# Paired column sums, bias rows on SP's queue and new rooms for accumulators in a two-layer decoder trunk

## The chip, the cores and the metric

The kernel runs on one core of a Trainium2 chip. The metric is the device time of one execution in microseconds (us). The program is compiled into one instruction stream for each engine: PE (TensorE: matrix products), DVE (VectorE), ACT (ScalarE), POOL (GpSimd) and SP (SyncE, which here only issues DMAs). An engine works through its own stream in order and waits at an instruction whose operands or whose output buffer are not ready.

## The reference

Two layers (D = 1024, 256 positions, hidden width 2816). Each layer is an FFN, a token mixer and a second FFN, and nine vectors of 1024 numbers, made from the conditioning vector `c`, modulate them. Vectors 0 and 1, 3 and 4, 6 and 7 are shift and scale of a norm; 2, 5 and 8 are the gates of the residual.

```
c_act = silu(c)
for l in range(2):
    mod = c_act @ w_ada[l] + b_ada[l]            # 9 vectors of 1024
    sh1, sc1, g1, sh2, sc2, g2, sh3, sc3, g3 = split(mod, 9)
    x = x + 0.5 * g1 * swiglu(rms_norm(x) * (1 + sc1) + sh1, ffn1_gate[l], ffn1_up[l], ffn1_down[l])
    x = x + g2 * token_mix(rms_norm(x) * (1 + sc2) + sh2, ...)
    x = x + 0.5 * g3 * swiglu(rms_norm(x) * (1 + sc3) + sh3, ffn2_gate[l], ffn2_up[l], ffn2_down[l])
return rms_norm(x) * final_norm
# swiglu(u, wg, wu, wd) = (silu(u @ wg) * (u @ wu)) @ wd
```

Everything is float32.

## The kernel before, in words

**Weights.** All weights stream in as `raw` tiles of 1 MB, issued by SP into four buffers (`raws`, bufs=4). A float32 weight is split in two: ACT copies it to `whi` (L177), DVE writes the remainder `wlo` (L179), and PE makes three products for each pair of operands: hi by hi, lo by hi and hi by lo. A `raw` buffer is free for the next load when its last reader is done: for a weight that is the second `wlo` split, for `w_ada` the last of DVE's four accumulations over it.

**FFN.** In the gate and up part, groups of 256 hidden columns follow each other (one `raw` tile of gate, one of up); DVE forms `hf` (L497) and its remainder `hl` (L499). In the down part two passes c = 0 and 1 run over six loads of `ffn_down`, each of which gives two *units*: one unit is one `whi` and one `wlo` of 128x1024 and twelve matmuls 128x512 of PE. At the end of a pass DVE adds the result to x (L455, L456, `rtmp`).

**Modulation.** The nine vectors are computed beside this work. A vector has two halves of 512 columns, a half has two loads of `w_ada` (1 MB each). `ada_half` issues them and lets DVE sum eight slices of 128x512 into a tile `acc` (L222 the first, L224 the others). For a gate the first of them adds the tile `binit`, whose row 0 holds the bias; that row of 2 KB is fetched by a DMA on ACT's queue (L212) in front of the half. What is left is a sum over the partitions, made by PE with a matrix of ones:

- a gate's half (a *row half*) is split into `acc0`, `acc1` (ACT L231, DVE L232), PE makes two matmuls 128x512 (`tr<-acc,ones`), ACT writes the gate `g` (L238);
- a half of a shift or scale (a *column half*) takes four matmuls of 32 columns in a bank `tr` (eight records in the trace), after which DVE picks the columns (L194 `mcol`, L197 `cs`) and adds the bias (L203 `col`).

`acc` has two buffers in the pool `keep`, which all halves use in turn. So a half can begin when PE has done the sums of the half before the last.

**Order.** `ada_step` goes one load further in this work; it is called between two loads of weights, once or twice for each group of the FFN and once for each load of `ffn_down`. The sums of a half are put one step after its last accumulation (`ada_late`). The tile framework's scheduler sets each engine's order at build time; at run time it is fixed.

The first two vectors of layer 0 and of layer 1's first FFN are made by another function. Layer 1's first FFN makes vectors 2, 3, 4 and 5 beside its groups and its down part: gate halves of vector 5 are summed in the down part.

Of the kernel before, what the change touches and what calls it, by code (L numbers as in the profile page):

```python
# [10 lines left out]
F32 = mybir.dt.float32  # L11
F32R = mybir.dt.float32r
AF = mybir.ActivationFunctionType
ALU = mybir.AluOpType
# [63 lines left out]
def hybrid_trunk(ctx, tc, t, out):  # L78
# [36 lines left out]
    pad(const, "before", 480)  # L115
# [4 lines left out]
    c_in = const.tile([P, KD], F32, name="c_in")  # L120
    nc.scalar.dma_start(c_in, t["c"].rearrange("o (p j) -> (o p) j", p=P))
    tab = const.tile([P, TAB_END], F32, name="tab")
# [3 lines left out]
    cact = const.tile([P, KD], F32, name="cact")  # L126
    nc.scalar.activation(cact, c_in, AF.Silu)
    apart = keep.tile([P, 48], F32, name="apart")
# [3 lines left out]
    pad(const, "behind", 352)  # L132
# [53 lines left out]
    def column_sums(ps, vec, a, start, stop):  # L186

        av = a.rearrange("p (j i r) -> p j i r", j=4, i=4)
        for i in range(4):
            mm(ps[32 * i:32 * i + 32, :P].rearrange("p (j r) -> p j r", j=4), vec, av[:, :, i, :], start, stop)  # L190

    def pick_columns(ps):
        m = small.tile([P, 4, 32], F32, name="mcol", tag="mcol", bufs=1)
        nc.vector.tensor_tensor(m, ps[:, :P].rearrange("p (j r) -> p j r", j=4),  # L194
                                colmask[:, None, :].to_broadcast([P, 4, 32]), ALU.mult)
        cs = small.tile([P, 4], F32, name="cs", tag="cs", bufs=2)
        nc.vector.tensor_reduce(cs, m, AX.X, ALU.add)  # L197
        return cs

    def add_bias(l, ch, n, cs):  # L200
        if (l, ch) not in mods:
            mods[l, ch] = small.tile([P, KD], F32, name="col", tag="col", bufs=8)
        nc.vector.scalar_tensor_tensor(mods[l, ch][:, n * 4:n * 4 + 4], cs, 1.0 if ch in (1, 4, 7) else 0.0,  # L203
                                       bcols[:, l, ch * 8 + n * 4:ch * 8 + n * 4 + 4], ALU.add, ALU.add)

    def ada_half(l, ch, n):
        acc = keep.tile([P, 512], F32, name="acc", tag="acc", bufs=2)
        row = ch in (2, 5, 8)
        n0 = ch * D + n * 512
        wv = t["w_ada"][l].rearrange("(p j) n -> p j n", p=P)  # L210
        if row:
            nc.scalar.dma_start(binit[0:1, :], t["b_ada"][l:l + 1, n0:n0 + 512])  # L212
        for j in range(0, KD, 4):
            r = raw_tile()
            rv = r.rearrange("p (j n) -> p j n", j=4)
            nc.sync.dma_start(rv, wv[:, j:j + 4, n0:n0 + 512])
            if ada_lag[0]:
                yield
            for jj in range(4):
                cj = cact[:, j + jj:j + jj + 1]  # L220
                if j + jj == 0 and not row:
                    nc.vector.tensor_scalar_mul(acc, rv[:, jj, :], cj)  # L222
                else:
                    nc.vector.scalar_tensor_tensor(acc, rv[:, jj, :], cj, binit if j + jj == 0 else acc,  # L224
                                                   ALU.mult, ALU.add)
            yield
        if row:
            if n == 0:
                mods[l, ch] = keep.tile([P, D], F32, name="g", tag="g", bufs=2)
            hi, lo = (scr.tile([P, 512], F32R, name="acc%d" % i, tag="uf", bufs=2) for i in range(2))  # L230
            nc.scalar.activation(hi, acc, AF.Copy)  # L231
            nc.vector.tensor_tensor(lo, acc, hi.bitcast(F32), ALU.subtract)  # L232

            def finish():
                ps = trps()
                mm(ps, ones, hi, True, False)
                mm(ps, ones, lo, False, True)
                nc.scalar.activation(mods[l, ch][:, n * 512:(n + 1) * 512], ps, AF.Copy, scale=1.0 if ch == 5 else 0.5)  # L238
        else:
            def finish():  # L240
                ps = trps()
                column_sums(ps, ones[:, :32].bitcast(F32), acc, True, True)
                cs = pick_columns(ps)
                add_bias(l, ch, n, cs)
        ada_late.append(finish)
# [5 lines left out]
    def ada_load(chunks):  # L251
        def g():
            for l, ch, n in chunks:
                for _ in ada_half(l, ch, n):
                    yield
                    while ada_late:
                        ada_late.pop(0)()
            while ada_late:
                ada_late.pop(0)()
        ada_gen[0] = g()  # L260
# [51 lines left out]
    def norm_mod(hf, uhi, ulo, sc, sh, by_act=False):  # L312
# [15 lines left out]
        def rest(bs=(0, 1)):  # L328
            for b in bs:
                uf = scr.tile([P, 4, P], F32, name="uf", tag="uf", bufs=2)  # L330
# [129 lines left out]
    def ffn(l, which, uhi, ulo, ada_plan, post, xn=None, side=None):  # L460
# [4 lines left out]
        with tc.tile_pool(name="ffn", bufs=1) as fp, tc.tile_pool(name="fu", bufs=EXTRA) as fu, \  # L465
# [7 lines left out]
            unit_alloc["f"] = lambda: pool_unit(fu)  # L473
            bank_pools[:] = [psum, fps]
# [26 lines left out]
            def begin():  # L501


                wa = t["w_ada"][l].rearrange("(p j) n -> p j n", p=P)
                cb = fp.tile([P, KD, 32], F32, name="cb", tag="sgx", bufs=2)
                nc.vector.tensor_copy(cb, cact[:, :, None].to_broadcast([P, KD, 32]))
# [40 lines left out]
                def operands(q):  # L547
                    cs = pick_columns(sums[q])
# [3 lines left out]
                    uf = scr.tile([P, 2, S], F32, name="uf", tag="uf", bufs=2)  # L552
# [64 lines left out]
            else:  # L617
                hidden()
                xs_group([(stream_units(wg[:, :, :512], KD, 512, 4, 2), 512, lambda hf, ps: gp.append(ps), 4),
# [29 lines left out]
            bank_pools[:] = [psum]  # L649


    def token_mix(l, uhi, ulo, ada_plan, post):
        uhk, ulk = ktiles(uhi), ktiles(ulo)
        w_in = t["w_in"][l].rearrange("(k p) n -> p k n", p=P)
        with tc.tile_pool(name="tm", bufs=1) as tp, tc.tile_pool(name="aps", bufs=2, space=PSUM) as aps:
# [58 lines left out]
            win = [scr.tile([P, 16, 2, 15], F32, name="win%d" % i, tag="uf", bufs=2) for i in range(2)]  # L714
# [259 lines left out]
            def transposed(blocks, eng):  # L974
# [4 lines left out]
                pT = scr.tile([P, 512], F32, name="pT", tag="uf", bufs=2)  # L979
# [142 lines left out]
    bcols = const.tile([P, DEPTH, 72], F32, name="bcols")  # L1122
# [18 lines left out]
    def final_norm(hf):  # L1141
        if hf == 0:
            for c in range(2):
                fnorm[c] = scr.tile([P, 512], F32, name="fnorm%d" % c, tag="uf", bufs=2)
# [18 lines left out]

    pad(scr, "before_uf", 320)
    pad(small, "behind_uf", 192)
# [57 lines left out]
```

## Time and profile before

| | |
|---|---|
| median of 3 runs | 1177.56 us (1176.16 to 1180.53) |
| the profiled execution | 1177.39 us, its span 1175.6 us |
| PE busy | 1145.2 us, 97% |
| DVE busy | 939.7 us, 80% |
| ACT busy | 642.8 us, 55% |
| granted TensorE clock | 0.999 |
| DMA on SP's queue | 273.02 MB, 70.8% of 16 engines' span |

Shares are means over stages that differ: what the change touches lies in the FFNs, and there the rows of single stretches count. A group of rows "x8" in a timeline is eight instructions in a row, its time from the start of the first to the end of the last. A matmul's time in the profile is modelled and overlaps the next; the pace of PE is read from the starts.

### The profile page before, as it was taken

How to read it: one execution, taken by the hardware profiler on the slowest of the kernel's cores; microseconds unless marked ns; L12 is line 12 of the kernel's file. 1: busy time of each engine (PE TensorE's matmuls, PEld its weight loads, DVE VectorE, ACT ScalarE, POOL GpSimd, SP SyncE). 2: the span in 40 equal slices, each digit the busy share in tenths (PEclk: the TensorE clock that was granted, in tenths of full speed). 3: DMA queues.
4: the chain of work that ended last, by engine and by line, in shares of the span. 5: the costliest groups of instructions: out<-in, count | busy, mean ns of one | idle time of the engine just before them, and what ended most of it. 6: DMA issues, size and time to landing. Idle time of an engine off the chain costs nothing.

```text
span 1175.6 us, 20207 instructions
## 1 busy us (share of the span) xinstructions
PE 1145.2 (97%) x7886; PEld 1005.6 (86%) x7886; DVE 939.7 (80%) x1889; ACT 642.8 (55%) x1156; POOL 2.6 (0%) x16
## 2 busy tenths in 40 slices
PE   4999999999999999999999999999999999999997
PEld 3799987799977889998879999777997788999985
DVE  4998899779888898799578879975888888865553
ACT  4544445647676564444455534365676757565441
POOL 0000000000000000000000000000000000000000
PEclk9999999999999999999999999999999999999999
DMA  9989999686723578988838979965574254986530
GB/s 329 333 294 318 329 342 354 203 231 184 220 80 104 193 232 297 314 290 318 287 108 289 321 266 347 342 230 165 154 225 114 88 180 143 294 267 210 188 135 36
DMA packets 201970, 274.95 MB, mean 234 GB/s; under 512 B 13613, under 2 KB 119815, under 8 KB 201875
## 3 DMA queue, kind: packets, MB, share of 16 engines
q1 hardware_dynamic: 201119, 273.02, 70.8%
q8 instruction: 62, 1.02, 0.4%
q10 hardware_dynamic: 756, 0.64, 0.2%
q14 instruction: 33, 0.27, 0.1%
HBM read 272.60 MB, written 1.05 MB: 233 GB/s over the span
## 4 chain that ended last, share of the span: by engine, by line
PE 64%; DVE 18%; DMA 11%; ACT 4%; issue 3%; SPq 1%; DVEq 0%; ACTq 0%
PE mm L105 55%; DVE wlo L179 8%; DMA raw<-in_ffn_up 6%; DVE acc L224 4%; PE tr L108 3%; DMA raw<-in_w_ada 3%; ACT whi L177 2%; PE sc L105 2%; PE po L105 2%; DMA raw<-in_ffn_down 1%; PE tr L105 1%; DVE win L728 1%; DMA raw<-in_ffn_gate 1%; DVE hf L497 1%; DVE rtmp L455 0%
## 5 line engine op out<-in xcount | busy, mean ns | idle before, releaser
L179 DVE TENSOR_TENSOR wlo<-raw,whi 128x1024 fp32r<-128x1024 f32 (+5 forms) x400 | 423.3, 1074 | 119.5 <-ACT whi L177 118.6
L177 ACT ACTIVATE whi<-raw 128x1024 fp32r<-128x1024 f32 (+5 forms) x400 | 364.4, 937 | 231.0 <-PE mm L105 92.8
L105 PE MATMUL mm<-uhi,whi 128*128 128x256 f32 x1248 | 346.6, 278 | 0.0
L105 PE MATMUL mm<-ulo,whi 128*128 128x256 f32 x1248 | 344.9, 276 | 0.0
L105 PE MATMUL mm<-uhi,wlo 128*128 128x256 f32 x1248 | 344.9, 276 | 0.0
L105 PEld LDWEIGHTS mm<-uhi,whi 128*128 128x128 f32 x1248 | 234.3, 188 | 2.7 <-issue 1.8
L105 PEld LDWEIGHTS mm<-ulo,whi 128*128 128x128 f32 x1248 | 234.5, 188 | 0.5
L105 PEld LDWEIGHTS mm<-uhi,wlo 128*128 128x128 f32 x1248 | 234.3, 188 | 0.0
L224 DVE SCALAR_TENSOR_TENSOR acc<-raw,cact,acc 128x512 f32<-128x512 f32 x224 | 167.3, 748 | 4.2 <-DMA raw<-in_w_ada 1.3
L105 PE MATMUL mm<-whi,hh 128*128 128x512 f32 x352 | 138.3, 393 | 0.0
L105 PE MATMUL mm<-wlo,hh 128*128 128x512 f32 x352 | 137.3, 390 | 0.7 <-DVE wlo L179 0.7
L105 PE MATMUL mm<-whi,hl 128*128 128x512 f32 x352 | 137.0, 389 | 0.0
L105 PE MATMUL mm<-whi,uhi 128*128 128x512 f32 (+3 forms) x336 | 126.4, 378 | 3.3 <-ACT uhi L557 2.6
L105 PE MATMUL mm<-whi,ulo 128*128 128x512 f32 (+3 forms) x336 | 126.0, 376 | 1.2 <-DVE ulo L345 1.2
L105 PE MATMUL mm<-wlo,uhi 128*128 128x512 f32 (+3 forms) x336 | 125.2, 373 | 0.0
L498 ACT ACTIVATE hh<-hf 128x256 fp32r<-128x256 f32 x70 | 29.3, 418 | 101.7 <-DVE hf L497 101.6
L105 PEld LDWEIGHTS mm<-whi,hh 128*128 128x128 f32 x352 | 66.1, 188 | 15.0 <-issue 1.4
L105 PEld LDWEIGHTS mm<-wlo,hh 128*128 128x128 f32 x352 | 66.1, 188 | 14.7 <-DVE wlo L179 1.4
L105 PEld LDWEIGHTS mm<-whi,hl 128*128 128x128 f32 x352 | 66.1, 188 | 13.8
L105 PEld LDWEIGHTS mm<-whi,uhi 128*128 128x128 f32 x336 | 63.3, 189 | 14.8 <-ACT uhi L557 3.3
L105 PEld LDWEIGHTS mm<-whi,ulo 128*128 128x128 f32 x336 | 63.7, 190 | 11.8 <-DVE ulo L345 2.9
L105 PEld LDWEIGHTS mm<-wlo,uhi 128*128 128x128 f32 x336 | 63.6, 189 | 9.4
(248 smaller groups left out, 1328.4 us busy)
## 6 DMA issues: line engine op xcount, KB each, us to landing
raw<-in_w_ada SPq DMA_DIRECT2D x72, 1024.0 KB, 7.9
raw<-in_ffn_gate SPq DMA_DIRECT2D x41, 1024.0 KB, 6.6
raw<-in_ffn_up SPq DMA_DIRECT2D x41, 1024.0 KB, 6.1
raw<-in_ffn_down SPq DMA_DIRECT2D x40, 1024.0 KB, 7.6
raw<-in_w_in SPq DMA_DIRECT2D x18, 1024.0 KB, 5.7
raw<-in_w_in SPq DMA_DIRECT2D x16, 512.0 KB, 4.7
raw<-in_w_out SPq DMA_DIRECT2D x8, 1024.0 KB, 5.4
raw<-in_ffn_down SPq DMA_DIRECT2D x8, 512.0 KB
```

Source lines behind the costliest of these rows:

```text
L105: last_mm[0] = nc.tensor.matmul(o, a, b, start=start, stop=stop)
L108: nc.tensor.transpose(o, a, ident)
L177: nc.scalar.activation(a, s, AF.Copy)
L179: nc.vector.tensor_tensor(b, s, a.bitcast(F32), ALU.subtract)
L224: nc.vector.scalar_tensor_tensor(acc, rv[:, jj, :], cj, binit if j + jj == 0 else acc, ALU.mult, ALU.add)
L497: nc.vector.tensor_tensor(hf32, ps[:, 256:], sg, ALU.mult)
L498: nc.scalar.activation(h[0][:, f, :], hf32, AF.Copy)
L728: nc.vector.tensor_tensor(win[i][jj * 64:(jj + 1) * 64, 8 * a:8 * a + 8, g, :], pv[g * 64:(g + 1) * 64, jj, :, a:a + 15], cols[0][jj * 64: ...
```

## The change

1. The two column halves of a vector are held and summed together: `column_sums` takes both accumulators and writes 256 columns of one bank, `mcol`, `cs` and `col` are made at double width, once for a vector. The sums come two steps after the second half; those of a row half one step after it, as before.
2. The bias row of a gate's half is fetched on SP's queue, by `bias_row`, which is called in the middle of the half before (for the first of all, in front of it). The tile `binit` is the same, so each fetch waits for DVE's accumulation that reads the row before it.
3. The accumulators of every second vector in an FFN (counter `pairs`, shift and scale only) go to a room of the FFN's pool, under the tag `sgx`, at other addresses; all others stay in `keep`'s two buffers. In the token mixer none goes there. With both halves held, a vector whose accumulators are in `keep` holds both buffers until its sums are done.
4. Tiles of the constants, `uf` and the paddings are laid out anew; SBUF offsets of some small tiles change.

```diff
-    def column_sums(ps, vec, a, start, stop):
-
-        av = a.rearrange("p (j i r) -> p j i r", j=4, i=4)
-        for i in range(4):
-            mm(ps[32 * i:32 * i + 32, :P].rearrange("p (j r) -> p j r", j=4), vec, av[:, :, i, :], start, stop)
...
+    def column_sums(ps, vec, halves):
+
+        for n, a in enumerate(halves):
+            av = a.rearrange("p (j i r) -> p j i r", j=4, i=4)
+            for i in range(4):
+                mm(ps[32 * i:32 * i + 32, n * P:(n + 1) * P].rearrange("p (j r) -> p j r", j=4), vec, av[:, :, i, :],
+                   True, True)
...
+    bias_order = [(l, ch, n) for l in range(DEPTH) for ch in (2, 5, 8) for n in range(2)]
+    bias_next = [0]
+
+    def bias_row():
+        if bias_next[0] < len(bias_order):
+            l, ch, n = bias_order[bias_next[0]]
+            bias_next[0] += 1
+            n0 = ch * D + n * 512
+            nc.sync.dma_start(binit[0:1, :], t["b_ada"][l:l + 1, n0:n0 + 512])
 
     def ada_half(l, ch, n):
-        acc = keep.tile([P, 512], F32, name="acc", tag="acc", bufs=2)
         row = ch in (2, 5, 8)
+        if not row and n == 0:
+            pairs[0] += 1
+        if not row and pairs[0] % 2 == 0 and acc_rooms[0] is not None:
+            acc = acc_rooms[0]()
+        else:
+            acc = keep.tile([P, 512], F32, name="acc", tag="acc", bufs=2)
         n0 = ch * D + n * 512
         wv = t["w_ada"][l].rearrange("(p j) n -> p j n", p=P)
-        if row:
-            nc.scalar.dma_start(binit[0:1, :], t["b_ada"][l:l + 1, n0:n0 + 512])
+        if row and bias_next[0] == 0:
+            bias_row()
         for j in range(0, KD, 4):
+            if row and j > 0:
+                bias_row()
             r = raw_tile()
...
         else:
+            held.append(acc)
+            if n == 0:
+                return
+            halves = list(held)
+            held.clear()
+
             def finish():
                 ps = trps()
-                column_sums(ps, ones[:, :32].bitcast(F32), acc, True, True)
-                cs = pick_columns(ps)
-                add_bias(l, ch, n, cs)
-        ada_late.append(finish)
+                column_sums(ps, ones[:, :32].bitcast(F32), halves)
+                cs = pick_columns(ps, KD)
+                mods[l, ch] = small.tile([P, KD], F32, name="col", tag="col", bufs=8)
+                nc.vector.scalar_tensor_tensor(mods[l, ch], cs, 1.0 if ch in (1, 4, 7) else 0.0,
+                                               bcols[:, l, ch * 8:ch * 8 + 8], ALU.add, ALU.add)
+        ada_late.append([1 if row else 2, finish])
...
+                    for e in list(ada_late):
+                        e[0] -= 1
+                        if e[0] == 0:
+                            ada_late.remove(e)
+                            e[1]()
...
+            acc_rooms[0] = lambda: fp.tile([P, 512], F32, name="acc", tag="sgx", bufs=2)
...
+            acc_rooms[0] = None
```

**PE, layer 1, first FFN, start of the down part.** Before: the sums of the second half of vector 4 stand alone, in front of the first unit of the pass (`whi_8276`).

```order
L105 MATMUL mm_8193<-ulo_6667,whi_8222 128x256
L105 MATMUL mm_8193<-uhi_6666,wlo_8223 128x256
L105 MATMUL tr_8260<-acc_7968,ones_83 32x128 x4
L105 MATMUL mm_8256<-whi_8276,hh_6763 128x512
L105 MATMUL mm_8256<-wlo_8277,hh_6763 128x512
```

Now both halves' sums, `acc_7647` and `acc_7935`, stand behind the second unit (`wlo_8239`) and in front of the third (`whi_8283`).

```order
L105 MATMUL mm_8212<-wlo_8239,hh_6730 128x512
L105 MATMUL mm_8212<-whi_8238,hl_6731 128x512
L105 MATMUL tr_8256<-acc_7647,ones_87 32x128 x4
L105 MATMUL tr_8256<-acc_7935,ones_87 32x128 x4
L105 MATMUL mm_8211<-whi_8283,hh_6730 128x512
```

Two groups of four for a vector have become one of eight, and this one moved behind two units of the down part.

**DVE, the same stretch.** Before, the first accumulation of vector 5 (`acc_8122<-...,binit_89`) stands in front of the splits of the first load of `ffn_down` (`wlo_8277`, `wlo_8293`).

```order
L224 SCALAR_TENSOR_TENSOR acc_8122<-raw_8124,cact_91,binit_89 128x512
L497 TENSOR_TENSOR hf32_8051<-mm_7992,sg_8049 128x256
L224 SCALAR_TENSOR_TENSOR acc_8122<-raw_8124,cact_91,acc_8122 128x512 x2
L499 TENSOR_TENSOR hl_6764<-hf32_8051,hh_6763 128x256
L224 SCALAR_TENSOR_TENSOR acc_8122<-raw_8124,cact_91,acc_8122 128x512
L179 TENSOR_TENSOR wlo_8277<-raw_8258,whi_8276 128x1024
L179 TENSOR_TENSOR wlo_8293<-raw_8258,whi_8292 128x1024
```

Now the same accumulation (`acc_8078<-...,binit_91`) stands behind the splits of the third load of `ffn_down` (`raw_8315`), and `acc_8078` and `acc_8276` are the same two buffers as `acc_7647` and `acc_7935` of vector 4.

```order
L181 TENSOR_TENSOR wlo_8329<-raw_8315,whi_8328 128x1024
L181 TENSOR_TENSOR wlo_8345<-raw_8315,whi_8344 128x1024
L530 TENSOR_TENSOR hf32_8207<-mm_8148,sg_8205 128x256
L532 TENSOR_TENSOR hl_6731<-hf32_8207,hh_6730 128x256
L245 SCALAR_TENSOR_TENSOR acc_8078<-raw_8079,cact_79,binit_91 128x512
L198 TENSOR_TENSOR mcol_8265<-tr_8256,tab_76 128x256
L245 SCALAR_TENSOR_TENSOR acc_8078<-raw_8079,cact_79,acc_8078 128x512
L201 TENSOR_REDUCE cs_8267<-mcol_8265 128x8
L245 SCALAR_TENSOR_TENSOR acc_8078<-raw_8079,cact_79,acc_8078 128x512
L272 SCALAR_TENSOR_TENSOR col_8269<-cs_8267,bcols_77 128x8
L245 SCALAR_TENSOR_TENSOR acc_8078<-raw_8079,cact_79,acc_8078 128x512
L245 SCALAR_TENSOR_TENSOR acc_8276<-raw_8277,cact_79,binit_91 128x512
```

Ten more accumulations into `acc_8078` and `acc_8276` follow, up to the remainder `acc1_8273` of the first of them. All accumulations of vector 5 moved behind six splits of the down part, with no split among the first fourteen.

**PE, the row sums of vector 5's first half.** Before, they stand between two units, behind the fourth unit of the pass (`whi_8339`) and in front of the fifth (`whi_8367`).

```order
L105 MATMUL mm_8257<-wlo_8340,hh_6763 128x512
L105 MATMUL mm_8257<-whi_8339,hl_6764 128x512
L105 MATMUL tr_8357<-acc0_8311,ones_83 128x512
L105 MATMUL tr_8357<-acc1_8312,ones_83 128x512
L105 MATMUL mm_8256<-whi_8367,hh_6763 128x512
```

Now they stand inside the sixth unit (`whi_8344`, `wlo_8345`), behind eight of its twelve matmuls.

```order
L105 MATMUL mm_8212<-whi_8344,hh_6730 128x512
L105 MATMUL mm_8212<-wlo_8345,hh_6730 128x512
L105 MATMUL tr_8317<-acc0_8272,ones_87 128x512
L105 MATMUL mm_8212<-whi_8344,hl_6731 128x512
L105 MATMUL mm_8212<-whi_8344,hh_6730 128x512
L105 MATMUL mm_8212<-wlo_8345,hh_6730 128x512
L105 MATMUL tr_8317<-acc1_8273,ones_87 128x512
L105 MATMUL mm_8212<-whi_8344,hl_6731 128x512
```

They moved from behind four units to the middle of the sixth.

## Rows read from the trace of the kernel before

**Rows 1.** The page's busy time: engine, us, share of the span, instructions.

```profile
PE 1145.2 (97%) x7886; PEld 1005.6 (86%) x7886; DVE 939.7 (80%) x1889; ACT 642.8 (55%) x1156; POOL 2.6 (0%) x16
```

**Rows 2.** Windows of us: length, each engine's busy time, clock, DMA share, GB/s.

```profile
700.00:735.00 35.00, 35.00 (x285) 33.11 (x284) 32.40 (x50) 17.30 (x27) 0.00 (x0) 1.00 0.99 352
735.00:780.00 45.00, 44.53 (x207) 35.84 (x207) 40.62 (x58) 21.66 (x29) 0.00 (x0) 1.00 0.94 323
```

**Rows 3.** Timeline of PE, one group of column sums: start, us, operation.

```profile
108.70 0.28 PE L105 MATMUL mm<-ulo,whi 128*128 128x256 f32 x1
108.82 0.28 PE L105 MATMUL mm<-uhi,wlo 128*128 128x256 f32 x1
109.02 0.42 PE L105 MATMUL tr<-acc,ones 128*32 128x128 f32 x8
109.38 0.39 PE L105 MATMUL mm<-uhi,whi 128*128 128x256 f32 x1
109.60 0.28 PE L105 MATMUL mm<-ulo,whi 128*128 128x256 f32 x1
```

**Rows 4.** Groups by line and form: count, busy us, mean ns, idle before.

```profile
L105 PE MATMUL tr<-acc,ones 128*32 128x128 f32 x160 | 8.5, 285 | 0.0
L194 DVE TENSOR_TENSOR mcol<-tr,tab 128x128 f32<-128x128 f32 x24 | 6.8, 285 | 0.1
L224 DVE SCALAR_TENSOR_TENSOR acc<-raw,cact,acc 128x512 f32<-128x512 f32 x224 | 167.3, 748 | 4.2 <-DMA raw<-in_w_ada 1.3
L177 ACT ACTIVATE whi<-raw 128x1024 fp32r<-128x1024 f32 x320 | 331.5, 1056 | 212.0 <-PE mm L105 74.8 <-DMA raw<-in_ffn_gate 49.1 <-DMA raw<-in_ffn_down 41.7
```

**Rows 5.** Timeline of SP, layer 1: issues of loads around the down part.

```profile
711.36 0.37 SPq L216 DMA_DIRECT2D raw<-in_w_ada  x1
717.53 0.37 SPq L216 DMA_DIRECT2D raw<-in_w_ada  x1
720.28 0.37 SPq L435 DMA_DIRECT2D raw<-in_ffn_down  x1
725.99 0.37 SPq L435 DMA_DIRECT2D raw<-in_ffn_down  x1
732.31 0.37 SPq L435 DMA_DIRECT2D raw<-in_ffn_down  x1
749.40 0.37 SPq L435 DMA_DIRECT2D raw<-in_ffn_down  x1
```

**Rows 6.** Timeline of DVE, layer 1, down part: first pass and start of the second.

```profile
720.17 0.74 DVE L224 SCALAR_TENSOR_TENSOR acc<-raw,cact,binit 128x512 f32<-128x512 f32 x1
720.83 0.42 DVE L497 TENSOR_TENSOR hf<-mm,sg 128x256 f32<-128x256 f32 x1
729.33 1.22 DVE L179 TENSOR_TENSOR wlo<-raw,whi 128x1024 fp32r<-128x1024 f32 x1
730.46 0.68 DVE L232 TENSOR_TENSOR acc<-acc,acc 128x512 fp32r<-128x512 f32 x1
735.76 2.35 DVE L179 TENSOR_TENSOR wlo<-raw,whi 128x1024 fp32r<-128x1024 f32 x2
...
758.77 2.36 DVE L179 TENSOR_TENSOR wlo<-raw,whi 128x1024 fp32r<-128x1024 f32 x2 [0.97 <-ACT whi L177]
...
765.28 0.68 DVE L455 TENSOR_TENSOR rtmp<-mm,g 128x512 f32<-128x512 f32 x1
```

**Rows 7.** Timeline of PE there: the fourth unit's first matmul, then the row sums.

```profile
735.97 0.39 PE L105 MATMUL mm<-whi,hh 128*128 128x512 f32 x1
738.69 0.61 PE L105 MATMUL tr<-acc,ones 128*128 128x512 f32 x2
739.14 0.39 PE L105 MATMUL mm<-whi,hh 128*128 128x512 f32 x1
```

**Rows 8.** Landing of loads: all of `ffn_down`, and 512 KB pieces (median us).

```profile
DMA to landing us min/median/max: 5.3/7.6/8.9
raw<-in_w_in SPq DMA_DIRECT2D x16, 512.0 KB, 4.7
```

More of the change, by code (lines that the diff above doesn't have):

```diff
@@ L114, in pad @@
         nc.gpsimd.memset(p, 0.0)
-    pad(const, "before", 480)
+    tab = const.tile([P, TAB_END], F32, name="tab")
+    bcols = const.tile([P, DEPTH, 72], F32, name="bcols")
+    c_in = const.tile([P, KD], F32, name="c_in")
+    cact = const.tile([P, KD], F32, name="cact")
+    pad(const, "before", 112)
     ident = const.tile([P, P], F32, name="ident")
@@ L119, in hybrid_trunk @@
     nc.scalar.activation(ones, ident, AF.Identity, scale=0.0, bias=1.0)
-    c_in = const.tile([P, KD], F32, name="c_in")
     nc.scalar.dma_start(c_in, t["c"].rearrange("o (p j) -> (o p) j", p=P))
-    tab = const.tile([P, TAB_END], F32, name="tab")
     nc.scalar.dma_start(tab[:, TAB_COL:TAB_END], t["tab"][:, TAB_COL:TAB_END])
@@ L125, in hybrid_trunk @@
     nc.gpsimd.memset(binit, 0.0)
-    cact = const.tile([P, KD], F32, name="cact")
     nc.scalar.activation(cact, c_in, AF.Silu)
+    nc.gpsimd.memset(keep.tile([P, 512], F32, name="uf", tag="uf", bufs=2)[:, :1], 0.0)
     apart = keep.tile([P, 48], F32, name="apart")
@@ L131, in hybrid_trunk @@
     colmask = tab[:, TAB_COL:TAB_COL + 32]
-    pad(const, "behind", 352)
+    pad(const, "behind", 192)
     def raw_tile():
@@ L184, in hybrid_trunk @@
     mods = {}
-    def column_sums(ps, vec, a, start, stop):
-        av = a.rearrange("p (j i r) -> p j i r", j=4, i=4)
-        for i in range(4):
-            mm(ps[32 * i:32 * i + 32, :P].rearrange("p (j r) -> p j r", j=4), vec, av[:, :, i, :], start, stop)
[L192 to L197, printed above, removed]
-        return cs
@@ L200, in add_bias @@
[L200 to L204, printed above, removed]
+    def column_sums(ps, vec, halves):
[4 more added lines that the diff above has]
+                   True, True)
@@ new lines, in pick_columns @@
+    def pick_columns(ps, n):
+        m = small.tile([P, KD, 32], F32, name="mcol", tag="mcol", bufs=1)
+        nc.vector.tensor_tensor(m[:, :n], ps[:, :n * 32].rearrange("p (j r) -> p j r", j=n),
+                                colmask[:, None, :].to_broadcast([P, n, 32]), ALU.mult)
+        cs = small.tile([P, KD], F32, name="cs", tag="cs", bufs=2)
+        nc.vector.tensor_reduce(cs[:, :n], m[:, :n], AX.X, ALU.add)
+        return cs
+    acc_rooms = [None]
+    pairs = [0]
+    held = []
@@ L229, in ada_half @@
                 mods[l, ch] = keep.tile([P, D], F32, name="g", tag="g", bufs=2)
-            hi, lo = (scr.tile([P, 512], F32R, name="acc%d" % i, tag="uf", bufs=2) for i in range(2))
+            hi, lo = (keep.tile([P, 512], F32R, name="acc%d" % i, tag="uf", bufs=2) for i in range(2))
             nc.scalar.activation(hi, acc, AF.Copy)
@@ L255, in g @@
                     yield
-                    while ada_late:
-                        ada_late.pop(0)()
+                    for e in list(ada_late):
[3 more added lines that the diff above has]
+                            e[1]()
             while ada_late:
-                ada_late.pop(0)()
+                ada_late.pop(0)[1]()
         ada_gen[0] = g()
@@ L329, in rest @@
             for b in bs:
-                uf = scr.tile([P, 4, P], F32, name="uf", tag="uf", bufs=2)
+                uf = keep.tile([P, 4, P], F32, name="uf", tag="uf", bufs=2)
                 ps = trps()
@@ L504, in begin @@
                 wa = t["w_ada"][l].rearrange("(p j) n -> p j n", p=P)
+                pad(fp, "before_sgx", 192)
                 cb = fp.tile([P, KD, 32], F32, name="cb", tag="sgx", bufs=2)
+                pad(fp, "behind_sgx", 320)
                 nc.vector.tensor_copy(cb, cact[:, :, None].to_broadcast([P, KD, 32]))
@@ L547, in operands @@
                 def operands(q):
-                    cs = pick_columns(sums[q])
+                    cs = pick_columns(sums[q], 4)
                     for i, ch in enumerate((1, 0)):
@@ L551, in operands @@
                                                        bcols[:, l, ch * 8 + q * 2:ch * 8 + q * 2 + 2], ALU.add, ALU.add)
-                    uf = scr.tile([P, 2, S], F32, name="uf", tag="uf", bufs=2)
+                    uf = keep.tile([P, 2, S], F32, name="uf", tag="uf", bufs=2)
                     for i in range(2):
@@ L618, in ffn @@
                 hidden()
+                pad(fp, "before_sgx", 192)
+                nc.gpsimd.memset(fp.tile([P, 512], F32, name="sgx", tag="sgx", bufs=2)[:, :1], 0.0)
+                pad(fp, "behind_sgx", 320)
                 xs_group([(stream_units(wg[:, :, :512], KD, 512, 4, 2), 512, lambda hf, ps: gp.append(ps), 4),
@@ L712, in token_mix @@
                 nc.vector.tensor_scalar_mul(cks[:, hf, :256], cks[:, hf, :256], lr[:, 2 + hf:3 + hf])
-            win = [scr.tile([P, 16, 2, 15], F32, name="win%d" % i, tag="uf", bufs=2) for i in range(2)]
+            win = [keep.tile([P, 16, 2, 15], F32, name="win%d" % i, tag="uf", bufs=2) for i in range(2)]
             r = raw_tile()
@@ L978, in transposed @@
                     tr(pt[:, c * P:(c + 1) * P], b)
-                pT = scr.tile([P, 512], F32, name="pT", tag="uf", bufs=2)
+                pT = keep.tile([P, 512], F32, name="pT", tag="uf", bufs=2)
                 if eng is nc.scalar:
@@ L1121, in hybrid_trunk @@
     nc.scalar.dma_start(brows, t["b_ada"].rearrange("l (a b) -> a l b", b=P))
-    bcols = const.tile([P, DEPTH, 72], F32, name="bcols")
     def bias_columns():
@@ L1143, in final_norm @@
             for c in range(2):
-                fnorm[c] = scr.tile([P, 512], F32, name="fnorm%d" % c, tag="uf", bufs=2)
+                fnorm[c] = keep.tile([P, 512], F32, name="fnorm%d" % c, tag="uf", bufs=2)
                 nc.scalar.dma_start(fnorm[c], t["final_norm"].rearrange("(o n) -> o n", o=1)
@@ L1162, in hybrid_trunk @@
         nc.vector.tensor_scalar(xn[hf], x[:, hf, :], r, a, ALU.mult, ALU.mult)
-    pad(scr, "before_uf", 320)
-    pad(small, "behind_uf", 192)
     def small_columns():
```

## The prediction

> **What bounds the kernel now.** The page's busy times come first: PE is busy for 1145.2 us, 97% of the span, DVE for 80% [rows 1]. So what shortens the run is work taken from PE, and what lengthens it is anything that makes PE wait. Next come the windows of the stretch in layer 1 where the order changed most. From 700 to 735 us PE is busy throughout, DVE for 32.40 of 35 us and the DMA engines for 0.99 of the time; from 735 to 780 us DMA is still at 0.94 [rows 2]. There is little room there: DVE and the loads are only a little ahead of PE, and time lost by either is not soon made up. Then the timelines of PE, SP and DVE in that stretch, for the distance between what PE needs and when it is made. The clock is 1.00 in both windows [rows 2], the 2.4 GHz level, and nothing here should move it.
>
> The profiled execution took 1177.39 us, 0.2 us under the median of 1177.56; sums start from 1177.4.
>
> **Column sums in pairs.** From the last matmul before a group to the second one after it, 108.82 to 109.60, is 0.78 us; undisturbed, two steps of 0.12 (108.70 to 108.82) would be 0.24. A group thus costs PE about 0.55 us, of which 0.36 lies between its first matmul and the next product [rows 3]. There are 160 records in groups of eight, so 20 groups [rows 4]. In a pair the second group repeats the eight records but not the gaps on both sides: 0.27, an estimate between the 0.36 and nothing (three quarters, as the last of its four matmuls already reaches into the gap). A pair then costs 0.82 instead of 1.10, 0.28 less. Of ten pairs, seven run as eight instructions in a row by PE's new order; the other three (vectors 6 and 7 of layer 0, vector 6 of layer 1) are pulled apart and gain nothing. Term: 7 x 0.28 = 2.0 us gained. Bounds: nothing, if the gaps stay with each group, and 20 x 0.55 / 2 = 5.5 us, if the second group cost nothing.
>
> The row shows that entering and leaving a group costs more than its instructions do. The Trainium skill (TensorEngine Tiling (Array Packing), Tiling Modes, Key Properties) states that a change of the tiling mode drains TensorE. The trace agrees in the 0.20 us from 108.82 to 109.02 [rows 3]; by that rule a pair pulled into three pieces pays one drain more than two groups did, and the sum would be 0.2 us worse for vector 6 of layer 0.
>
> **DVE's share of it.** Ten `mcol` of 0.285 us [rows 4] go, and the other ten double in width; a 128x256 operation on the same engine takes 0.42 [rows 6]. That is 0.15 less a pair, and the same again at most for `cs` and `col`: up to 3 us of DVE over the run. Beside PE's work it is hidden; I count nothing for it, and 0 to 3 us as bounds.
>
> **Bias rows on SP's queue.** ACT loses twelve issues. SP issues a 1 MB load in 0.37 us [rows 5] and is mostly waiting for buffers, so the issue itself is hidden. What is not hidden is the wait: each fetch waits until DVE has read the row before it, and all loads of weights stand behind it. Where the reading accumulation comes early this is nothing. In layer 0's down part one fetch holds the next `w_ada` load back, by an estimate one transfer of 1 MB at 352 GB/s [rows 2], 3.0 us; that delays accumulations and not splits. I count 0, with 0 to 3 as bounds. In layer 1's down part it stands in front of the fourth `ffn_down` load, but that load waits for a buffer longer anyway (below).
>
> **New offsets.** The same accumulation takes 0.74 us reading `binit` and 0.748 reading `acc` [rows 4, 6], though the two lie at different offsets. I count nothing for the layout; bounds 3 us either way.
>
> **Layer 1, from groups to down part.** This is the term that decides. The sums of vector 4 now come two units late, and both of `keep`'s buffers are held until then: vector 4 of layer 1 is the ninth pair, an odd one, so it is in `keep`. Vector 5 needs the same two buffers. Before, its first accumulation began at 720.17 [rows 6], between the last splits of the groups. Now it stands behind the splits of three `ffn_down` loads.
>
> First the loads. Three `w_ada` loads (issued before at 711.36, 717.53 and a third after them [rows 5]) sit unread in three of the four `raw` buffers until that accumulation. All `ffn_down` loads then go through one buffer, one after another. The second is issued at 720.28 as before and split from 729.33 [rows 5, 6]; two splits back to back take 2.35 [rows 6], thus the third can go at 731.7 instead of 725.99. It lands after 5.3 us at the shortest, 7.6 in the median [rows 8]; with fewer transfers in flight I take 6.0, so 737.7. ACT's two copies at 1.06 [rows 4] and the last split of 1.2 [rows 6] bring both splits to 741.0.
>
> Then DVE's queue, in order: `hf` and `hl` (records of 0.42 that overlap [rows 6], some 0.7 for both, 741.7), then fourteen accumulations, `mcol`, `cs`, `col` and the remainder `acc1`. Accumulations into alternate buffers step at 0.66 (720.17 to 720.83 [rows 6]); 14 x 0.66 = 9.2. With 0.75 for the three small ones and 0.68 for the remainder (730.46 [rows 6]): 741.7 + 9.2 + 0.75 + 0.68 = 752.3.
>
> PE meets the row sums after five and two thirds units. A unit takes 2.72 us (735.97 to 738.69); the fourth ended at 738.69 and would end about there again, the pair's 0.8 us put in and one single group and other savings taken out [rows 7]. The fifth needs the first split of the third load, at 737.7 + 1.06 + 1.2 = 740.0, so it ends at 742.7; eight matmuls of the sixth take 1.8, and PE stands at the row sums from 744.5. It waits until 752.3: **7.8 us**, where before `acc1` was made at 730.46 + 0.68, 7.5 us ahead of its use at 738.69 [rows 6, 7].
>
> Bounds of this wait: with the third load's splits at 738.1 as before (735.76 + 2.35 [rows 6]) the same queue ends at 749.4, PE is there at 743.2, and the wait is 6.2; with accumulations at 0.748 it is 1.2 more, 9.0; a later landing delays both. None at all needs these splits done by 743.2 - 11.3 = 731.9.
>
> What is late next: the fourth `ffn_down` load, issued at 732.31 before [rows 5], waits for the buffer of the first `w_ada`, four accumulations into the queue, at 741.7 + 3.4 = 745.1. It lands at 751.1 and its first split is done at 753.4, 0.6 us after PE has finished the sixth unit. The split after it stands behind an accumulation whose `w_ada` load could go only when the second buffer was read, twelve accumulations in, near 749.7, and so lands near 756: about 2 us more, and another 0.9 at the next load. By 749.40 SP had issued the seventh `ffn_down` load in the pass's order [rows 5]; now it is three behind. In DVE's new order the additions to x at the end of the first pass (765.28 before, behind the first splits of the second pass, which began at 758.77 [rows 6]) stand in front of those splits: up to 0.6 + 0.6 + 0.6 + 1.2 = 3 us more at the turn. All this together is 0 to 6.5 us; I take 3, because each part hangs on a landing of 6.0 that may be 5.3.
>
> A check by bytes: DMA moves 352 GB/s there [rows 2], 1 MB in 3.0 us. From 731.7 to 745 it could move 4.4 loads and moves two or so: some 7 us of transfer are lost in a stretch that is 0.99 full. That agrees with a slip of 7 us and more.
>
> A small one in the same place: the second bias row is fetched when the first is read, near 742, and needed three us later. The nearest landing shown is 4.7 us for 512 KB [rows 8]; taken whole it would add 2 us to the wait, and I leave it in the range. The Trainium skill (DMA: Bandwidth & Descriptors, Anatomy of one DMA) gives a fixed cost of about 2.0 us a DMA, by which the row would be there in time and add nothing; no row here shows the landing of 2 KB.
>
> **The sum.** 1177.4 - 2.0 + 7.8 + 3.0 = 1186.2, with the rest at 0. PE has no slack behind it to give the time back: after this it is bound by its own matmuls again.
>
> **Rivals.** *A, no wait there.* Place: the third load's splits. If a buffer comes free earlier than I read it, so that the splits are done by 731.9, the burst is hidden and only the pairs' gain remains: 1177.4 - 2.0 = 1175.4; half of the wait would give 1179.3. For it: before, the same accumulations had 7.5 us to spare. Against it: DVE's order is fixed, and the third load can't be issued before the second is split. *B, faster.* If the gaps go wholly (5.5), and 3 us of DVE's relief go to stretches in which DVE limits, with A: 1177.4 - 5.5 - 3 = 1169 to 1172. For it: DVE at 32.40 of 35 us [rows 2]; against it: PE was busy in all 35 of them. *C, the queue blocks more.* SP's fetches hold weights back in layer 0 too (3 us), the bias row lands late (2) and the turn costs its whole (3.5 more): 1186.2 + 8.5 = 1194.7. *The pairs stay apart*: then the gain of 2.0 goes and 1188.2 remains, inside the forecast's own range.
>
> **How the numbers follow.** The forecast has 0.57 (its own range 1181 to 1191.5), A 0.25 (1174 to 1181), B 0.11, C 0.07. A measurement can tell 0.5% or 5.9 us from no change, so the limits are 1171.7 and 1183.4. Faster is B, most of it: 0.10. The same is A and the forecast's low end (0.07): 0.32. Slower is the rest: 0.58. The range leaves out B's faster half and C's end: 1172 to 1193.
>
> **What would show it.** In the profile after: PE idle for 5 to 11 us near 744 to 752 us in one piece, ended by DVE's `acc1` remainder; DVE's first accumulation of vector 5 near 741 instead of 720.17; the third `ffn_down` load issued near 732; DMA below 0.7 from 732 to 745; groups of sixteen records `tr<-acc`, 0.63 us from the first to the next product. The prediction is wrong if that wait is under 3 us, or if more than 4 us appear or go elsewhere.

## The result, and where the time went

The changed kernel takes 1195.40 us in the median of 5 runs (1193.62 to 1196.83), against 1178.10 for the kernel before: a ratio of 1.0129, 95% interval 1.0104 to 1.0154. It is slower, as forecast, but by 17.3 us where 8.8 had been worked out, and beyond the range. The profiled execution took 1195.28 us.

Where it is lost is read best from PE: the start of the same product in both traces, after less before. This lag is not a view of its own; it is worked out from the two timelines, each of a single execution.

| stretch (us of before) | lag at its end | added | what stands there |
|---|---|---|---|
| 0 to 60 | 1.4 | 1.4 | granted clock 0.84 from 20 to 40 us |
| 60 to 170 | 2.3 | 0.9 | pairs of column sums, a slower step of the products |
| 170 to 210 | 5.65 | 3.4 | layer 0's first down part, fetches of bias rows |
| 210 to 300 | 6.8 | 1.2 | start of layer 0's token mixer |
| 300 to 735 | 7.0 | 0.2 | |
| 735 to 785 | 18.0 | 11.0 | layer 1's first down part |
| 785 to the end | 17.9 | 0 | |

The place is the one the prediction named. DVE's timeline of the changed kernel there (start, us, operation, idle before it in brackets) answers to [rows 6]:

```profile
740.81 2.36 DVE L181 TENSOR_TENSOR wlo<-raw,whi 128x1024 fp32r<-128x1024 f32 x2 [4.99 <-ACT whi L179]
...
744.33 0.74 DVE L245 SCALAR_TENSOR_TENSOR acc<-raw,cact,binit 128x512 f32<-128x512 f32 x1
...
748.04 0.76 DVE L245 SCALAR_TENSOR_TENSOR acc<-raw,cact,binit 128x512 f32<-128x512 f32 x1 [0.19 <-DMA binit<-in_b_ada]
748.71 6.18 DVE L245 SCALAR_TENSOR_TENSOR acc<-raw,cact,acc 128x512 f32<-128x512 f32 x9
754.80 0.68 DVE L253 TENSOR_TENSOR acc<-acc,acc 128x512 fp32r<-128x512 f32 x1
```

The first accumulation of vector 5 has moved from 720.17 to 744.33, behind the splits of the third `ffn_down` load; that load could be issued only at 734.60, where 731.7 was forecast and 725.99 had been [rows 5]:

```profile
723.98 0.37 SPq L467 DMA_DIRECT2D raw<-in_ffn_down  x1
734.60 0.37 SPq L467 DMA_DIRECT2D raw<-in_ffn_down  x1
747.88 0.37 SPq L467 DMA_DIRECT2D raw<-in_ffn_down  x1
```

PE meets it inside the sixth unit, where [rows 7] had no gap:

```profile
750.02 0.39 PE L105 MATMUL mm<-wlo,hh 128*128 128x512 f32 x1
754.65 0.79 PE L105 MATMUL tr<-acc,ones 128*128 128x512 f32 x1 [4.24 <-ACT acc L252]
755.24 0.63 PE L105 MATMUL mm<-whi,hl 128*128 128x512 f32 x1
755.67 0.63 PE L105 MATMUL mm<-whi,hh 128*128 128x512 f32 x1
...
760.24 0.39 PE L105 MATMUL mm<-wlo,hh 128*128 128x512 f32 x1
760.47 0.39 PE L105 MATMUL mm<-whi,hl 128*128 128x512 f32 x1
```

PE waits 4.24 us, and then the products step at 0.43 us instead of 0.23 until 759.94. The windows (columns as in [rows 2]) show what goes with it: the granted clock falls to 0.50, the lower of its two levels, 1.2 GHz.

```profile
745.00:750.00 5.00, 5.00 (x23) 4.13 (x23) 4.81 (x10) 0.00 (x0) 0.00 (x0) 1.00 0.71 215
750.00:755.00 5.00, 0.76 (x3) 0.35 (x2) 4.96 (x9) 1.98 (x3) 0.00 (x0) 0.82 0.66 218
755.00:760.00 5.00, 5.00 (x13) 3.83 (x13) 4.95 (x7) 1.78 (x3) 0.00 (x0) 0.50 1.05 392
775.00:780.00 5.00, 4.03 (x11) 2.87 (x12) 4.89 (x7) 4.97 (x9) 0.00 (x0) 0.71 0.83 307
```

PE is "busy" for all of 755 to 760 and does 13 instructions where 23 are usual. The wait and the slow stretch give 7.1 us of lag; another 3.9 come at the turn of the two passes, at 775 us, with waits of 2.03 and 0.69 us and a second fall of the clock.

```profile
775.28 0.73 PE L105 MATMUL mm<-whi,hh 128*128 128x512 f32 x2 [2.03 <-ACT whi L179]
776.70 0.50 PE L105 MATMUL mm<-wlo,hh 128*128 128x512 f32 x1 [0.69 <-DVE wlo L181]
```

### The profile page after: what moved, and what is told of

Read it like the earlier page. It is cut to its first block, busy times and chain, and to the rows that moved or that the text cites. A ratio compares the mean times of both kernels' runs of the same rounds, so it can differ in the third digit from the quotient of the medians.

```text
span 1193.5 us, 20195 instructions
## 1 busy us (share of the span) xinstructions
PE 1153.0 (97%) x7886; PEld 1012.1 (85%) x7886; DVE 939.2 (79%) x1859; ACT 642.0 (54%) x1156; POOL 3.3 (0%) x26
## 4 chain that ended last, share of the span: by engine, by line
PE 63%; DVE 16%; DMA 13%; ACT 5%; issue 3%; SPq 1%; DVEq 0%; ACTq 0%
PE mm L105 54%; DVE wlo L181 7%; DMA raw<-in_ffn_up 5%; DMA raw<-in_ffn_down 3%; DMA raw<-in_w_ada 3%; PE tr L108 3%; ACT whi L179 3%; DVE acc L245 3%; PE sc L105 2%; PE po L105 2%; DMA raw<-in_ffn_gate 2%; PE tr L105 1%; DVE win L767 1%; ACT junk L328 0%; DVE rtmp L487 0%
```

## The experiments

**The other room.** In the kernels with this edit vectors 3 and 4 of layer 1 change rooms.

```diff
-        if not row and pairs[0] % 2 == 0 and acc_rooms[0] is not None:
+        if not row and (pairs[0] % 2 == 0) != (l == 1 and ch in (3, 4)) and acc_rooms[0] is not None:
```

> Of layer 1's vectors 3 and 4 the rooms are swapped: vector 4 goes to the FFN's pool, vector 3 to keep. Theory (the two held buffers make the wait): the first accumulation of vector 5 moves back in front of the down part's splits, PE's wait of 4.2 us at the row sums and the half-speed stretch behind it go, and so do the 2.0 + 0.7 us at the turn of the passes; 11 us less than the changed kernel, about 1184.5 us. Rival (the fetch of the bias row on SP's queue holds the loads back): the lag in layer 1's down part stays above 6 us, 1190 us or more.

Measured: 1182.29 us, ratio to before 1.0029 (1.0008 to 1.0050), 13.1 us under the changed kernel. The first accumulation is back in front of the down part's splits, the row sums of vector 5's first half stand between two units without a wait:

```profile
721.22 0.74 DVE L245 SCALAR_TENSOR_TENSOR acc<-raw,cact,binit 128x512 f32<-128x512 f32 x1
...
735.31 0.69 DVE L253 TENSOR_TENSOR acc<-acc,acc 128x512 fp32r<-128x512 f32 x1
...
742.42 0.62 PE L105 MATMUL tr<-acc,ones 128*128 128x512 f32 x2
```

The lag of that down part is 0.9 us (3.72 to 4.62, from 735 to 785 us of before) instead of 11.0. The held buffers made the wait; the rival falls.

**Bias rows on ACT again.**

```diff
-        if row and bias_next[0] == 0:
-            bias_row()
+        if row:
+            nc.scalar.dma_start(binit[0:1, :], t["b_ada"][l:l + 1, n0:n0 + 512])
...
-            if row and j > 0:
-                bias_row()
```

> The changed kernel with the bias rows fetched on ACT's queue in front of each half, as before. Theory (buffers): layer 1's wait stays within 2 us of its 11; only the 3.4 us that layer 0's down part lost (170 to 205 us) come back, about 1192 us. Rival (queue): layer 1's lag falls by more than half, below 1187 us.

Measured: 1191.73 us, ratio 1.0100 (1.0077 to 1.0123), 3.7 us under the changed kernel in the medians. The lag at 200 us is 1.5 instead of 5.65. What the fetches did is seen in SP's timeline of the changed kernel, in layer 0's down part (before, a load of `w_ada` went there at 149.46):

```profile
148.76 0.37 SPq L467 DMA_DIRECT2D raw<-in_ffn_down  x1
155.91 0.27 SPq L218 DMA_DIRECT2D binit<-in_b_ada  x1
156.23 0.37 SPq L237 DMA_DIRECT2D raw<-in_w_ada  x1
156.70 0.45 SPq L467 DMA_DIRECT2D raw<-in_ffn_down  x1
```

SP stood at the 2 KB fetch for 6.8 us, until 155.91, with a `w_ada` load and a weight load behind it. With the bias rows on ACT's queue the same two loads go 4.9 and 2.5 us earlier:

```profile
151.34 0.37 SPq L235 DMA_DIRECT2D raw<-in_w_ada  x1
154.17 0.37 SPq L465 DMA_DIRECT2D raw<-in_ffn_down  x1
```

Over the run of the changed kernel SP waits 41.3 us at such fetches (total, times, longest):

```profile
SPq L218 <- DVE acc L245: 41.3, 11, 6.9
```

DMA's share from 150 to 200 us is 0.92 in the changed kernel and 0.98 here. In layer 1 the wait is still there, and longer, because PE is no longer late when it comes to it:

```profile
753.98 0.79 PE L105 MATMUL tr<-acc,ones 128*128 128x512 f32 x1 [7.55 <-ACT acc L250]
```

That is near the forecast's 7.8 us. The median came as the theory said, but the condition did not hold: the down part's lag is 14.6 us here, 3.6 more than the changed kernel's 11.0, where 2 were allowed. The profiled execution, the slowest of the four at 1195.15 us, takes as long as the changed kernel's 1195.28: the longer wait takes back what the fetches gave. So what the fetches cost is better read from the next experiment.

**Both.** The two edits together.

> Both edits together: vector 4 of layer 1 in the other room and the bias rows on ACT's queue. Theory: the two losses add, 1195.4 - 11 - 3.4 = 1181 us. Rival (one of them hides the other): 1184 us or more, as with the room alone.

Measured: 1178.77 us, ratio 0.9996 (0.9984 to 1.0007). 16.6 us go, where the two alone give 13.1 and 3.7: they add, and nothing measurable is left of the loss. The kernel before measured 1178.10 us beside the changed kernel and 1179.34 beside these three, so differences between these three are the safer ones: 3.5 us for the fetches (1182.29 less 1178.77) and 13.0 for the room (1191.73 less 1178.77). By place, the kernel with the other room alone, which keeps the fetches, loses against the one with both edits 1.2 us from 40 to 85, 1.7 from 180 to 200 and 2.0 in layer 1's down part; 0.7 of the 1.2 is a slower step of 173 products from 66 us (below), not a wait. The 3.4 us of the changed kernel's trace in layer 0's down part are partly chance: the kernel with the other room has the same order on every engine up to 300 us and loses 0.75 there.

**The layout alone.** Halves summed singly, all accumulators in `keep`, bias rows on ACT.

```diff
-        ada_late.append([1 if row else 2, finish])
+        ada_late.append([1, finish])
```

(besides the edit above, and `column_sums` and `pick_columns` called for one half).

> The changed kernel with halves summed one by one, all accumulators in keep and bias rows on ACT's queue: what is left of the change is where the tiles lie. Theory (the layout costs nothing): 1178 us, within 1.5 us of before; the 128x256 products step at 113 to 114 ns throughout the groups. Rival (the layout slows PE, with a step of 118 ns in the last two groups and 1.5 us lost before 40 us): 1181 to 1183 us.

Measured: 1180.61 us, ratio 1.0012 (0.9994 to 1.0030): no difference that can be told. In its profile the products start at 113 ns behind every group of sums in the FFNs; one stretch turns to 118 in its middle, at 721.02, where PE waited 0.28 us. It also shows 2.1 us of lag by 34 us, with the clock at 0.91 from 20 to 40 us. These are much like the rival's two signs, but the kernel of the next experiment has the same layout, steps at 113 in all these groups behind sums and lost nothing at the start, so the layout alone does not make them. The start loss stays open.

**The fetches alone.** The same with `bias_row` on SP.

> The layout-alone kernel with only the bias rows moved to SP's queue. Theory (each fetch that waits for DVE holds the loads behind it back, with or without pairs): the lag grows at the places of the fetches, near 60 to 80 us and in both first FFNs' down parts, 3 us or more in all, about 1183 to 1184 us against 1180.6 of the layout alone. Rival (the queue blocks only where the pairs delay DVE's reading of the row): within 1 us of the layout alone.

Measured: 1182.42 us, ratio 1.0023 (1.0004 to 1.0042), 1.8 us over the layout alone, with overlapping intervals. In the traces the lag grows against the layout alone by 1.3 us from 40 to 85, 1.3 at 180 to 200, 1.2 at 560 and 2.1 at 760 to 770, while its start was 2.4 us better. The second and the last stand in down parts with fetches, with sizes near those between the other room and both edits; of the first, 0.7 is the slower step of 173 products from 65.70 us again; at 560 no fetch is near (445.31 and 616.53), and what was lost there stays open. So by the traces the fetches cost in the down parts without pairs too; that they cost 3 us in the run's time is not shown by these medians.

**Sums a step earlier.** The changed kernel with one expression changed:

```diff
-        ada_late.append([1 if row else 2, finish])
+        ada_late.append([1, finish])
```

> The changed kernel with a pair's sums one step behind its second half instead of two. Theory (what makes the wait is that both of keep's buffers are held until the pair's sums, which PE reaches only with the down part): the first accumulation of vector 5 still stands behind five splits of the down part, PE waits at the row sums behind the fourth unit for 8 us or more, and the time is within 4 us of the changed kernel's 1195.4. Rival (the second step of delay makes it): the lag of layer 1's down part falls below 4 us, under 1188 us.

Measured: 1191.82 us, ratio 1.0101 (1.0066 to 1.0136). The wait is 6.14 us near the fourth unit, the down part's lag 9.5. So it is the holding, not the second step, that decides; the wait came out under the 8 us expected.

**A filled wait.** The kernel with bias rows on ACT, and in front of layer 1's first row sums:

```diff
+                if (l, ch, n) == (1, 5, 0):
+                    for _ in range(44):
+                        mm(ps, ones, warm[0], True, True)
```

> The changed kernel with bias rows on ACT's queue (the one that waited 7.55 us at layer 1's row sums) with 44 products 128x512 without use in front of these row sums, 10.0 us of work in the wait; the order has the row sums behind the fourth unit then, so the wait itself is longer, some 12 us. Theory (the clock fell because PE stood idle): the granted clock stays at 1.00 through the wait and behind it, where it was 0.74 and 0.50. Rival (it falls for another cause in that stretch): below 0.9 again from 745 to 760 us.

Measured once: 1190.08 us. First the windows of the kernel that waited idle, then its own, then its timeline with the products without use:

```profile
745.00:755.00 10.00, 2.45 (x9) 1.68 (x8) 9.89 (x17) 2.52 (x3) 0.00 (x0) 0.74 0.64 228
755.00:760.00 5.00, 5.00 (x13) 3.93 (x12) 5.00 (x7) 1.43 (x3) 0.00 (x0) 0.50 1.04 395
```

```profile
745.00:755.00 10.00, 9.19 (x39) 6.89 (x38) 9.75 (x14) 2.53 (x3) 0.00 (x0) 1.00 0.67 237
755.00:760.00 5.00, 5.00 (x24) 4.14 (x23) 4.93 (x8) 3.13 (x4) 0.00 (x0) 1.00 1.06 379
```

```profile
740.98 10.43 PE L105 MATMUL tr<-uhi,ones 128*128 128x512 f32 x44
```

The clock stays at 1.00. The down part's lag is 10.6 us instead of 14.6, though PE does 10 us of work more before the row sums: the idle wait cost more than itself (its row sums stand nearly two units earlier than in the kernel that waited idle). The Trainium skill (TensorE: Matmul & The Clock Gate, What's actually happening) says that the throttled clock is the default state and that activity lifts it; the windows of the idle and the filled wait agree. Not every wait brings the clock down: 2.17 us in the kernel with the fetches alone (at 771.61) and 1.40 in the one with sums a step earlier (at 774.88) left it at 1.00.

**The slow step.** Behind the pairs the 128x256 products run slower: 172 records in 20 us, where the kernel before has 178, 118 ns for one instead of 113. The windows are of the changed kernel, and of before in the same groups:

```profile
134.00:154.00 20.00, 20.00 (x172) 20.00 (x171) 19.05 (x30) 9.21 (x15) 0.00 (x0) 1.00 0.96 335
```

```profile
110.00:130.00 20.00, 20.00 (x178) 20.00 (x178) 17.49 (x29) 7.72 (x12) 0.00 (x0) 1.00 0.95 308
```

Three stretches of 192 such products lie behind pairs, at 3.9 ns each (20/172 less 20/178) some 2.3 us. Is it the group of sixteen records? In the kernel before, each half's sums were issued twice:

```diff
-                column_sums(ps, ones[:, :32].bitcast(F32), acc, True, True)
+                for _ in range(2):
+                    column_sums(ps, ones[:, :32].bitcast(F32), acc, True, True)
```

> The kernel before with each half's four column sums issued twice into the same bank (same values), so that groups of sixteen records stand alone, without pairs, held accumulators or other rooms. Theory (a group of sixteen records leaves the 128x256 products behind it at a step of 118 ns instead of 113): all stretches of 128x256 products behind such a group in the FFNs run at 118 until the next 128x512 product, some 0.4 us for each 96. Rival (the slow step comes from held accumulators or from where they lie): they stay at 113 to 114, and the run is only the 20 x 0.13 us of the repeated records longer.

Measured once: 1183.88 us. Behind the first such group (108.53 us) the products step at 118 ns, behind the second (131.92) at 113, behind the third (143.59) at 118 again:

```profile
110.00:130.00 20.00, 20.00 (x172) 20.00 (x171) 17.72 (x29) 7.80 (x13) 0.00 (x0) 1.00 0.92 296
133.00:143.00 10.00, 10.00 (x90) 10.00 (x90) 9.96 (x18) 4.51 (x7) 0.00 (x0) 1.00 1.01 338
145.00:155.00 10.00, 10.00 (x88) 10.00 (x87) 8.71 (x16) 3.58 (x6) 0.00 (x0) 1.00 1.03 378
```

Held accumulators and rooms are ruled out, but the expectation was only half right: the group does not slow the products, it switches between two steps. In each of three FFNs the groups between such products give 118, 113, 118 in turn.

**Alternating order**, `for i in range(4)` outside and the halves inside, on the kernel with both edits.

> The kernel with the other room and ACT's queue, with a pair's eight sums in alternating order (first half, second half, for each of the four column positions). Theory (the number of records sets the slow step): 118 ns behind each pair as before. Rival (the order of column positions sets it): 113 to 114 ns behind the pairs, 2.5 us less lag in the three first FFN parts together.

Measured once: 1179.49 us. Two of the three stretches are at 118 throughout; the first goes back to 113 after 123 of 192 products, behind a short wait of PE for a weight's remainder:

```profile
146.24 0.39 PE L105 MATMUL mm<-uhi,wlo 128*128 128x256 f32 x1 [0.32 <-DVE wlo L181]
```

The order of columns does not set it.

**A wide product behind each pair.**

```diff
+                if wide[0] is not None:
+                    mm(trps(), ones, wide[0], True, True)
```

> The kernel with the other room and ACT's queue, with one 128x512 product without use (ones by the normed input) behind each pair in the FFNs. Theory (a 128x512 product ends the slow step): 113 to 114 ns behind the pairs, 0.84 us less in each of three stretches for 0.3 to 0.45 us more at each of eight pairs, so about the same time, 1178 to 1180 us, with the step restored. Rival (it is not the PE's state): 118 ns stays, and the run is 2.5 to 3.5 us longer.

Measured: 1180.41 us, ratio 1.0008 (0.9996 to 1.0021). All three stretches are at 118. That theory fell, and with the switching seen above a third was made: each eight records beyond the first switch once.

**Three groups.** The first half's sums twice in each pair, 24 records:

```diff
-        for n, a in enumerate(halves):
+        for n, a in [(0, halves[0])] + list(enumerate(halves)):
```

> The kernel with the other room and ACT's queue, with the first half's four sums issued twice in each pair (same values), so that a group has 24 records instead of 16. Theory (a group of sixteen switches the step of the 128x256 products between 113 and 118 ns, a group of eight leaves it; so each eight beyond the first switches it once, and 24 leave it): 113 to 114 ns behind all pairs in the FFNs, 2.5 us less for 8 x 0.13 us more, about 1177 us. Rival (any group over eight switches it): the same three stretches at 118, about 1180 us.

Measured: 1178.57 us, ratio 0.9989 (0.9971 to 1.0008). No stretch behind the FFNs' pairs is slow (179 records in 20 us):

```profile
133.00:153.00 20.00, 20.00 (x179) 20.00 (x178) 18.85 (x30) 8.63 (x14) 0.00 (x0) 1.00 0.99 341
```

The step came out as expected; the 2.5 us did not show in the run's time, and this kernel can't be told from the kernel before.

## Why the prediction was wrong

**Layer 1, from groups to down part: right in place and mechanism.** Order and loads are as worked out, and DMA's share from 732 to 745 us is 0.38. The releaser is not: PE waited for ACT's `acc0`, not for DVE's remainder `acc1`. PE's row sums take `acc0` first, and in ACT's order it stands behind a copy of the fourth `ffn_down` load:

```profile
753.02 1.06 ACT L179 ACTIVATE whi<-raw 128x1024 fp32r<-128x1024 f32 x1 [9.07 <-DMA raw<-in_ffn_down]
753.99 0.61 ACT L252 ACTIVATE acc<-acc 128x512 fp32r<-128x512 f32 x1
```

The remainder was ready at 755.48, and PE took it at 756.52 without a wait. By the forecast's own terms that load's copy ends at 751.1 + 1.06 = 752.2, so both paths gave the same end, and that the size came out is partly luck. The wait forecast at 7.8 us is 7.55 with the bias rows on ACT, where PE comes only some 2 us late. In the changed kernel it is 4.24, because PE came to the row sums at 750.25 instead of 744.5, 5.75 us late by losses elsewhere, while they were released only 2.4 us late (754.65 for 752.3).

**"The clock is 1.00 in both windows, the 2.4 GHz level, and nothing here should move it": this step failed.** A wait was added and its effect on PE's clock was not. With bias rows on ACT the wait of 7.55 us gave 10.7 of lag, thus 3.1 more at the lower clock; at the turn 3.9, of which waits are about 2.7. So the 3.0 put down for what is late next was about right for the waits, and some 4 us of clock were missing. All of those waits stand at the turn; at the fourth load, where the forecast had 0.6 and its own terms give 0.2 (752.3 and four matmuls are 753.2, against 753.4), PE did not wait. The filled wait shows the cause.

**"That delays accumulations and not splits; I count 0": this step failed too.** The fetches cost 3.7 us in the changed kernel by the medians, and 3.5 beside the other room. The bounds of 0 to 3 came near; the value taken was the wrong end. The reason given left out that SP's queue is one line: behind the fetch stood not one `w_ada` load but a weight load too, the one 4.9 us late instead of 3, the other 2.5.

**The pairs' gain of 2.0 us did not come.** A pair needs what was estimated: from the first of sixteen records to the next product are 0.58 us, 0.22 more than for eight, where 0.27 was put down, so the gaps on both sides are paid once, as the drain of the Trainium skill (TensorEngine Tiling (Array Packing), Tiling Modes, Key Properties) would have it. But the products behind three of the pairs ran 3.9 ns slower each, 2.3 us in sum. None of the rows read showed this: behind every group of sums in the FFNs of before the products step at 113.

```profile
132.85 0.64 PE L105 MATMUL tr<-acc,ones 128*32 128x128 f32 x16
133.43 0.38 PE L105 MATMUL mm<-uhi,whi 128*128 128x256 f32 x1
```

**Layout at 0: not contradicted.** The start of the run, 1.4 us, and the token mixer, 1.2 us, were not forecast. The second is in all nine kernels with pairs (0.6 to 1.5 us from 250 to 300) and in neither of the two with this layout and single halves; what in the pairs makes it was not tried. The first is in the profiled executions of three of the eleven kernels with this layout, each time with a lower clock before 34 us; its cause is open.

Sum: the forecast had -2.0 + 10.8 = +8.8. By the runs it is 13.1 for the room, 3.7 for the fetches, and about 0.5 for the rest. In the trace layer 1's down part has 11.0 of the 17.9, about 7 of it waits and most of the rest clock. Of the rivals, C had the right kind of addition (the queue, the turn) and came within 1 us, 1194.7, for parts of its reasons; that it came so near is luck, since it has no clock and its late bias row, put at 2 us, cost 0.19 us of DVE's time (the row's fetch was issued at 745.10, and DVE read it at 748.04). A and B fell.

## What to carry to other kernels

When two results are held so that they can be finished together, look for who needs their buffers next, and where in each engine's order the finish stands: the saving is fractions of a microsecond, the wait is the length of a burst. An added wait on a PE that was never idle can cost more than its length: behind 4.2, 6.1 and 7.6 us, and behind 2.03 and 0.69 close together, the clock fell here. A transfer that waits for a reader does not belong at the head of the queue that feeds everything else, however small it is.

## What was not expected of the hardware

The 128x256 products have two steady steps, 113 and 118 ns, at a granted clock of 1.00, and keep either for as many as 288 products. In all the traces together, each group of sixteen records of 32 columns that stood alone between such products changed the step, 32 times to the slower and 4 times back. Groups of 24 (3) and of 8 (37) behind the faster step left it. A 128x512 product behind the group did not restore it.

These groups are not the only switch. In the kernel before, 72 products at 118 ns stand in the token mixer:

```profile
832.50:840.50 8.00, 8.00 (x70) 8.00 (x70) 7.73 (x26) 5.19 (x9) 0.31 (x1) 1.00 0.69 223
```

There too the products before the group of eight at 265.75 step at 118 and those behind it at 113. In the kernels with the other room alone and with the fetches alone, 173 products from 66 us run at 118 with no group of sums in front of them. And where PE waited a little inside a stretch (0.28 to 0.60 us between two starts), the step changed three times from 118 to 113, once from 113 to 118 (the layout alone, at 721.02), and three times it stayed at 113. What inside PE it is, no run here shows.
